# Order of the block loads in the feed-forward units, and two operand differences on VectorE

## The chip, the cores and the metric

The kernel runs on one core of a Trainium2 chip. The core has TensorE (matrix products), VectorE, ScalarE and GpSimd (elementwise work), SyncE (here only the queue that issues DMA transfers) and 16 DMA engines between HBM and the on-chip memory. The metric is the device time of one execution in microseconds.

## The reference, cut to what matters

The kernel computes one trunk layer of a decoder. 520 token columns (512 of a prompt, 8 of single-token sequences) go through norms, projections, two kinds of attention, and a feed-forward part. Only the last is touched by the change:

```python
D_MODEL = 2048
D_FF = 4 * D_MODEL
h = rmsnorm(x) * (1 + scale2) + shift2
x = x + gate2 * rmsnorm(relu(h @ w_ff1) ** 2 @ w_ff2)
```

All inputs are float32, and both matrix products are computed to nearly full float32 accuracy.

## The kernel before, in words

**Three matmuls for one product.** TensorE multiplies a shortened type. Each operand is therefore cut into a high part (ScalarE's cast) and a low part (the operand less its high part), and a block product is high·high + high·low + low·high: `mm3`, lines 445 to 447, matmuls of 128x128 by 260 columns. For weights the cut is `split_staged`: ScalarE casts (line 430, tile `wh`), ScalarE copies the block into PSUM (line 435, tile `stg`), VectorE subtracts (line 436, tile `wl`). For activations it is `split1` (lines 326 and 327, tiles `xf`).

**Units.** Most of both feed-forward products runs as units. A unit is a 2x2 block product done in seven block products rather than eight, by Strassen's scheme in Winograd's form. `PRODS` gives their order: P1 (weight A11), P5 (S1), P6 (S2), P3 (S4), P7 (S3), P2 (A12), P4 (A22). The A are 128x1024 blocks of weights (512 KB each); the S are sums of them, made by GpSimd in `wsum` (line 373):

S1 = A21 + A22, S2 = S1 − A11, S4 = A12 − S2, S3 = A11 − A21.

The other operand of each product is made of activations: B11, B22, B21 and T1 to T4, where T1 = B12 − B11, T2 = B22 − T1, T3 = B22 − B12, T4 = B21 − T2. Each product is 24 matmuls, a unit 168.

**Stages.** The first matrix has 28 units, two tiles of 128 output rows each; its result goes through relu and square (`ff1_unit`, tiles `fr`) to DRAM. The second matrix has 28 units, seven chunks of the hidden dimension with four units each (`ff2_unit`); an eighth chunk follows in a plain form. For a chunk, `form` loads four activation blocks from DRAM (line 2055, tiles `st`) and makes B and T (lines 2049 and 327). `form(0)` runs during the last unit of the first matrix; `form(c + 1)` runs step by step during chunk c.

**What sets the order.** Every engine runs its instructions in the order in which they were written. `drive` lists, for each unit, its four blocks (`items`), its sums (`sumq`) and its products (`subs`). `sub` is called once per product: it issues loads up to seven items ahead, then the sums that are due, then the cuts of the next products. Blocks of kind "unit" go into a pool of four buffers (`wr`), those of kind "more" into other slots (`wr2`; three in the second matrix). Both matrices list A11, A12 as "unit" and A21, A22 as "more". A load waits in SP's queue until its buffer has been read for the last time. In the second matrix A21's buffer is the one that the previous unit's S3 reads last; the buffers of the others are freed by ScalarE's cuts. `load_to(k + 3)` in `wsum` sees to it that all four blocks are issued before any sum is. `form` for c > 0 pins its instructions to their written place among the others (`keep_in_program_order`); `form(0)` doesn't.

Of the kernel before, what the change touches and what calls it, by code (L numbers as in the profile page):

```python
# [13 lines left out]
OP = mybir.AluOpType  # L14
# [53 lines left out]
RING = 6  # L68


PRODS = (("P1", "A11", "B11", 0, True), ("P5", "S1", "T1", 1, True), ("P6", "S2", "T2", 0, False),
         ("P3", "S4", "B22", 1, False), ("P7", "S3", "T3", 0, False), ("P2", "A12", "B21", 2, True),
         ("P4", "A22", "T4", 0, False))
# [163 lines left out]
class Kern:  # L237
# [92 lines left out]
    def drive(self, ops):  # L330

        self.items, self.subs, self.sumq = [], [], []
        for items, _ in ops:
            k = len(self.items)
            self.items += items
            if items and items[0][1] == "unit":
                for _, src, *_ in PRODS:
                    if src[0] == "S":
# [26 lines left out]

    def wsum(self, k, name):

        a, b, op = {"S1": (2, 3, OP.add), "S2": ("S1", 0, OP.subtract), "S3": (0, 2, OP.subtract),
                    "S4": (1, "S2", OP.subtract)}[name]
        self.load_to(k + 3)  # L370
        a, b = (self.sums[k, n] if isinstance(n, str) else self.raw[k + n] for n in (a, b))
        t = self.sums[k, name] = self.V1.tile([128, 1024], F32, name=name, tag="s")
        self.nc.gpsimd.tensor_tensor(t, a, b, op=op)  # L373

    def sub(self):

        i = self.isub
        k, _, _, now = self.subs[i]
        for d in (self.raw, self.sums):
            for key in [key for key in d if (key[0] if d is self.sums else key) < k]:  # L380
                del d[key]
        look = 7 if isinstance(now, str) else 4 if self.items[min(k + 4, len(self.items) - 1)][1] == "more" else 2
        self.load_to(k + (LOOK if self.items[min(k + LOOK, len(self.items) - 1)][1] == "ada" else look))
        while self.sumq and self.sumq[0][0] <= i + 2 + SL:
            _, ku, name = self.sumq.pop(0)
            self.wsum(ku, name)
        while self.icut < len(self.subs) and (self.icut <= i + 2 or self.ahead < 3):
            k, o, n, src = self.subs[self.icut]
            if src and self.icut > i and sum(self.held.values()) + self.need(n) > RING:
                break  # L390
            if self.icut > i and self.items[k][1] == "more" and not self.more:
                break
            if self.icut > i + 2 and self.items[k][1] == "ada":
                break
            if not src:
                self.load_to(k)
                self.cut[self.icut] = self.raw[k]
            else:
                if src is True or src[0] == "A":
                    k += 0 if src is True else ("A11", "A12", "A21", "A22").index(src)  # L400
                    self.load_to(k)
                    wr = self.raw[k][:, o:o + n]
                else:
                    wr = self.sums[k, src][:, o:o + n]
                self.held[self.icut] = self.need(n)
                if n > 512 and self.slot % 2:
                    self.slot = (self.slot + 1) % RING
                a = 512 * self.slot
                self.slot = (self.slot + (n + 511) // 512) % RING
                wh, wl = self.wh[:, a:a + n], self.wl[:, a:a + n]  # L410
                if n > 512 and self.stage:
                    self.split_staged(wr, wh, wl)
                else:
                    self.split1(wr, wh, wl)
                self.cut[self.icut] = (wh, wl)
                self.ahead += 1
            self.icut += 1
        self.isub += 1
        self.ahead -= bool(now)
        self.held.pop(i, None)  # L420
        return self.cut.pop(i)
# [1551 lines left out]
    def products(self, deep, done):  # L1973


        accs = {}
        for name, _, x, c, opens in PRODS:
            if opens:
# [13 lines left out]
    def ff1_unit(self, t):  # L1992
        def run():
# [17 lines left out]
            def done(name, acc):  # L2011
# [13 lines left out]

            self.products(True, done)
        w = self.I["wff1"]
        return [(w[t][:, :1024], "unit"), (w[t][:, 1024:], "unit"), (w[t + 1][:, :1024], "more"),
                (w[t + 1][:, 1024:], "more")], run

    def step_form(self, last=True):

# [11 lines left out]
    def form(self, c):  # L2044

        pin = self.tc.keep_in_program_order if c else lambda ins: ins

        def tt(*a, **k):
            pin(self.nc.gpsimd.tensor_tensor(*a, **k))  # L2049

        order = ((0, 0), (0, 1), (1, 1), (1, 0))
        st = []
# [24 lines left out]
        if c:  # L2077
            yield 3
        tt(b11, b12, b11, op=OP.subtract)
        if c:  # L2080
            yield 2
        t2 = self.V1.tile([128, 4, HF], F32, name="t2", tag="a")
        tt(t2, b22, b11, op=OP.subtract)
        if c:
            yield 2
        put("T1", b11, pool)
        if c:
            yield 3
        tt(b12, b22, b12, op=OP.subtract)
        if c:  # L2090
            yield 2
# [51 lines left out]
    def ff2_unit(self, c, g):  # L2143
# [19 lines left out]

            self.products(False, done)
        w = self.I["wff2"][c, g]
        return [(w[b], "unit" if b < 2 else "more") for b in range(4)], run

    def open_last(self):
        self.close_fc()
# [108 lines left out]
```

## Time and profile before

| | us |
|---|---|
| three runs | 2857.93, 2870.22, 2874.36 |
| median | 2870.22 |
| the profiled execution | 2863.88 |
| its span | 2862.2 |
| TensorE busy (share of the span) | 2689.3 (94%) |
| VectorE busy | 1691.0 (59%) |
| ScalarE busy | 1571.3 (55%) |
| GpSimd busy | 1141.2 (40%) |

The span runs from the first to the last instruction; the execution's own time holds 1.7 us more around it. The units of the first matrix begin at about 1557 us and end at about 2126, those of the second run from 2135 to 2738, and the plain chunk and the last norm end at 2862. The mean granted clock of TensorE is 0.975 of its full level of 2.4 GHz; at the lower level, 1.2 GHz, a matmul takes twice as long. A row of a timeline reads: start, duration, engine, line, operation, output and inputs, and in brackets the idle time before it with what ended it. Matmuls are pipelined: the distance of their starts is what one costs, not the duration shown.

### The profile page before, as it was taken

To read this page: it belongs to the slowest core of one execution; us is meant where nothing else is said; L and a number is where in the kernel's file an instruction comes from. 1 tells how busy PE (TensorE), PEld (TensorE's weight loads), DVE (VectorE), ACT (ScalarE), POOL (GpSimd) and SP (SyncE) were. 2 spreads that over 40 slices of the span, in tenths; PEclk is the share of its full clock that TensorE was granted. 3 is DMA by queue.
4 is the path that set the end of the run, shared out by engine and by line. 5 is a ranking of instruction groups with operands and counts; after the bars stand their busy time and mean duration, and the time that the engine had idled before them with its cause. 6 is when DMAs were issued, how large, how long until landed. Compare 5 with 4: busy or idle time off the path is not lost.

```text
span 2862.2 us, 56309 instructions
## 1 busy us (share of the span) xinstructions
PE 2689.3 (94%) x21584; PEld 2490.1 (87%) x21584; DVE 1691.0 (59%) x3336; ACT 1571.3 (55%) x2780; POOL 1141.2 (40%) x909
## 2 busy tenths in 40 slices
PE   6999998999999989899988999999989999999996
PEld 3589967788888878788978999999989999999996
DVE  4465483357594555623886555555565666665667
ACT  3134322234544434323565777777778777777773
POOL 0000011113113351301554665655667676776613
PEclk9999999999999999899998999999999999999998
DMA  7753456754445546677655434334342333323354
GB/s 259 284 172 78 123 183 200 223 184 140 159 155 166 177 144 199 198 245 262 232 170 177 145 118 143 124 136 137 127 153 92 119 120 143 123 98 139 131 181 155
DMA packets 195126, 466.15 MB, mean 163 GB/s; under 512 B 25609, under 2 KB 76170, under 8 KB 194858
## 3 DMA queue, kind: packets, MB, share of 16 engines
q1 hardware_dynamic: 165616, 421.83, 43.5%
q10 hardware_dynamic: 27194, 36.53, 4.3%
q0 software_dynamic: 2048, 4.21, 0.5%
q8 instruction: 170, 2.79, 0.4%
q14 instruction: 98, 0.80, 0.1%
HBM read 413.57 MB, written 48.91 MB: 162 GB/s over the span
## 4 chain that ended last, share of the span: by engine, by line
PE 53%; DVE 8%; POOL 6%; issue 5%; ACT 4%; DMA 4%; SPq 0%; ACTq 0%; POOLq 0%; DVEq 0%
PE acc L445 16%; PE acc L447 15%; PE acc L446 15%; POOL S L373 3%; DMA wr<-in_wff 2%; PE m L480 2%; DMA wr<-in_win 2%; ACT wh L430 2%; DVE wl L327 1%; POOL xf L327 1%; DVE wl L436 1%; ACT stg L435 1%; PE m L274 1%; PE m L1139 1%; POOL st L2049 1%
## 5 line engine op out<-in xcount | busy, mean ns | idle before, releaser
L436 DVE TENSOR_TENSOR wl<-stg,wh 128x512 fp32r<-128x512 f32 (+1 forms) x584 | 490.0, 867 | 407.8 <-ACT wh L430 396.4
L445 PE MATMUL acc<-hh,wh 128*128 128x260 f32 (+1 forms) x1984 | 587.0, 297 | 10.9 <-ACT hh L621 4.9
L446 PE MATMUL acc<-hl,wh 128*128 128x260 f32 (+1 forms) x1984 | 567.7, 287 | 0.4 <-DVE hl L622 0.4
L447 PE MATMUL acc<-hh,wl 128*128 128x260 f32 (+1 forms) x1984 | 565.2, 286 | 1.3 <-DVE wl L327 1.3
L445 PE MATMUL acc<-xf,wh 128*128 128x260 f32 x1824 | 521.1, 286 | 24.7 <-ACT stg L435 20.4
L326 ACT CAST wh<-wr 128x512 fp32r<-128x512 f32 (+1 forms) x478 | 284.1, 612 | 467.4 <-DMA wr<-in_win 220.4
L327 DVE TENSOR_TENSOR wl<-wr,wh 128x512 fp32r<-128x512 f32 (+1 forms) x478 | 353.5, 754 | 312.9 <-ACT wh L326 304.4
L447 PE MATMUL acc<-xf,wl 128*128 128x260 f32 x1824 | 518.5, 284 | 4.6 <-DVE wl L327 4.6
L446 PE MATMUL acc<-xf,wh 128*128 128x260 f32 x1824 | 518.3, 284 | 0.0
L445 PEld LDWEIGHTS acc<-hh,wh 128*128 128x128 f32 (+1 forms) x1984 | 376.0, 190 | 85.5 <-issue 45.5
L446 PEld LDWEIGHTS acc<-hl,wh 128*128 128x128 f32 (+1 forms) x1984 | 376.6, 190 | 8.0 <-DVE hl L622 4.5
L447 PEld LDWEIGHTS acc<-hh,wl 128*128 128x128 f32 (+1 forms) x1984 | 375.8, 190 | 5.9 <-DVE wl L327 4.4
L373 POOL TENSOR_TENSOR S<-wr,wr 128x1024 f32<-128x1024 f32 x112 | 276.4, 2469 | 252.7 <-DMA wr<-in_wff 170.9
L445 PEld LDWEIGHTS acc<-xf,wh 128*128 128x128 f32 x1824 | 346.7, 190 | 28.2 <-ACT stg L435 25.9
L447 PEld LDWEIGHTS acc<-xf,wl 128*128 128x128 f32 x1824 | 346.7, 190 | 4.9 <-DVE wl L327 4.9
L446 PEld LDWEIGHTS acc<-xf,wh 128*128 128x128 f32 x1824 | 346.6, 190 | 0.0
L435 ACT COPY stg<-S 128x512 f32<-128x512 f32 (+1 forms) x334 | 240.7, 731 | 106.2 <-DVE wl L436 73.1
L447 PE MATMUL acc<-h2h,wl 128*128 128x260 f32 x928 | 266.3, 287 | 8.8 <-DVE wl L327 8.7
L445 PE MATMUL acc<-h2h,wh 128*128 128x260 f32 x928 | 266.1, 287 | 6.2 <-ACT h2h L326 3.7
L446 PE MATMUL acc<-h2l,wh 128*128 128x260 f32 x928 | 266.4, 287 | 4.5 <-DVE h2l L327 4.5
L445 PE MATMUL acc<-T,wh 128*128 128x260 f32 x896 | 255.9, 286 | 11.6 <-DVE fr L2007 8.9
L447 PE MATMUL acc<-T,wl 128*128 128x260 f32 x896 | 256.0, 286 | 2.0 <-DVE wl L327 2.0
(538 smaller groups left out, 5800.8 us busy)
## 6 DMA issues: line engine op xcount, KB each, us to landing
wr<-in_wff SPq DMA_DIRECT2D x256, 512.0 KB, 4.8
wd<-in_wada SPq DMA_DIRECT2D x106, 512.0 KB, 4.7
wr<-in_win SPq DMA_DIRECT2D x106, 512.0 KB, 4.5
wr<-in_wada SPq DMA_DIRECT2D x86, 512.0 KB, 3.9
wr<-in_wout SPq DMA_DIRECT2D x48, 512.0 KB, 4.6
st<-f SPq DMA_DIRECT2D x32, 520.0 KB, 5.3
pg<-in_ckt SPq DMA_DIRECT2D x256, 64.0 KB, 2.7
wr<-in_wff2l SPq DMA_DIRECT2D x32, 512.0 KB, 3.5
```

The costliest lines, as they stand in the source:

```text
L274: self.nc.tensor.transpose(out, in_, self.ident[:n, :n])
L326: pin(self.nc.scalar.copy(hh, x))
L327: pin((eng or self.nc.vector).tensor_tensor(hl, x, hh.bitcast(F32), op=OP.subtract))
L373: self.nc.gpsimd.tensor_tensor(t, a, b, op=op)
L430: nc.scalar.copy(hh, x)
L435: nc.scalar.copy(p, x[:, s])
L436: nc.vector.tensor_tensor(hl[:, s], p, hh[:, s].bitcast(F32), op=OP.subtract)
L445: T.matmul(acc, wh[:, cs], xh, start=first, stop=False, skip_group_check=goes_on)
L446: T.matmul(acc, wh[:, cs], xl, start=False, stop=False, skip_group_check=goes_on)
L447: T.matmul(acc, wl[:, cs], xh, start=False, stop=last, skip_group_check=goes_on)
L480: self.nc.tensor.matmul(self.aacc[v][32 * g:32 * g + 32, :], self.cs[:, kt, :], w[:, j * 512:(j + 1) * 512], start=(kt == 0), stop=(kt == ...
L1139: nc.tensor.matmul(po[:, 0:256], vt[:, kb_ + k], pts[:, 256 * k:256 * k + 256], start=(kb_ + k == 0), stop=(kb_ + k == i))
```

## The change

It has two parts.

The four blocks of a unit are listed as A21, A22, A11, A12 instead of A11, A12, A21, A22, so that A21 and A22 go into the pool `wr` and A11 and A12 into the slots `wr2`. `UNIT` holds this order. A sum asks only for the blocks that it reads itself: `wsum` calls `load_to` with the larger index of its own blocks, no longer with the fourth.

In `form(0)` the first two differences, T1 = B12 − B11 and T2 = B22 − T1, go to VectorE instead of GpSimd. The third and fourth, and all of the later chunks, stay on GpSimd.

```diff
--- before.py
+++ after.py
@@ -68,6 +68,7 @@
 RING = 6
 
 
+UNIT = ("A21", "A22", "A11", "A12")
 PRODS = (("P1", "A11", "B11", 0, True), ("P5", "S1", "T1", 1, True), ("P6", "S2", "T2", 0, False),
          ("P3", "S4", "B22", 1, False), ("P7", "S3", "T3", 0, False), ("P2", "A12", "B21", 2, True),
          ("P4", "A22", "T4", 0, False))
@@ -365,10 +366,10 @@
 
     def wsum(self, k, name):
 
-        a, b, op = {"S1": (2, 3, OP.add), "S2": ("S1", 0, OP.subtract), "S3": (0, 2, OP.subtract),
-                    "S4": (1, "S2", OP.subtract)}[name]
-        self.load_to(k + 3)
-        a, b = (self.sums[k, n] if isinstance(n, str) else self.raw[k + n] for n in (a, b))
+        a, b, op = {"S1": ("A21", "A22", OP.add), "S2": ("S1", "A11", OP.subtract),
+                    "S3": ("A11", "A21", OP.subtract), "S4": ("A12", "S2", OP.subtract)}[name]
+        self.load_to(k + max(UNIT.index(n) for n in (a, b) if n in UNIT))
+        a, b = (self.raw[k + UNIT.index(n)] if n in UNIT else self.sums[k, n] for n in (a, b))
         t = self.sums[k, name] = self.V1.tile([128, 1024], F32, name=name, tag="s")
         self.nc.gpsimd.tensor_tensor(t, a, b, op=op)
 
@@ -397,7 +398,7 @@
                 self.cut[self.icut] = self.raw[k]
             else:
                 if src is True or src[0] == "A":
-                    k += 0 if src is True else ("A11", "A12", "A21", "A22").index(src)
+                    k += 0 if src is True else UNIT.index(src)
                     self.load_to(k)
                     wr = self.raw[k][:, o:o + n]
                 else:
@@ -2025,8 +2026,8 @@
 
             self.products(True, done)
         w = self.I["wff1"]
-        return [(w[t][:, :1024], "unit"), (w[t][:, 1024:], "unit"), (w[t + 1][:, :1024], "more"),
-                (w[t + 1][:, 1024:], "more")], run
+        return [(w[t + 1][:, :1024], "unit"), (w[t + 1][:, 1024:], "unit"), (w[t][:, :1024], "more"),
+                (w[t][:, 1024:], "more")], run
 
     def step_form(self, last=True):
 
@@ -2046,7 +2047,7 @@
         pin = self.tc.keep_in_program_order if c else lambda ins: ins
 
         def tt(*a, **k):
-            pin(self.nc.gpsimd.tensor_tensor(*a, **k))
+            pin((self.nc.gpsimd if c else self.nc.vector).tensor_tensor(*a, **k))
 
         order = ((0, 0), (0, 1), (1, 1), (1, 0))
         st = []
@@ -2086,6 +2087,8 @@
         put("T1", b11, pool)
         if c:
             yield 3
+        else:
+            tt = self.nc.gpsimd.tensor_tensor
         tt(b12, b22, b12, op=OP.subtract)
         if c:
             yield 2
@@ -2163,7 +2166,7 @@
 
             self.products(False, done)
         w = self.I["wff2"][c, g]
-        return [(w[b], "unit" if b < 2 else "more") for b in range(4)], run
+        return [(w[b], kind) for b, kind in ((2, "unit"), (3, "unit"), (0, "more"), (1, "more"))], run
 
     def open_last(self):
         self.close_fc()
```

Lines from 71 on have one number more after the change, those from line 2092 on three more.

**SP's queue in the second matrix, before.** The loads of two units, the second being the first of a chunk. The pairs `wr_27721`, `wr_27723` and `wr_27988`, `wr_27990` are A11 and A12; the pairs `wr2_27725`, `wr2_27727` and `wr2_27992`, `wr2_27994` are A21 and A22. The `st` are the activation blocks of the next chunk.

```order
L362 DMA wr_27721<-in_wff2 128x1024
L362 DMA wr2_27725<-in_wff2 128x1024
L362 DMA wr_27723<-in_wff2 128x1024
L362 DMA wr2_27727<-in_wff2 128x1024
L362 DMA wr_27988<-in_wff2 128x1024
L362 DMA wr2_27992<-in_wff2 128x1024
L2055 DMA st_27979<-f400_14719 128x1040
L2055 DMA st_27981<-f401_14720 128x1040
L362 DMA wr_27990<-in_wff2 128x1024
L2055 DMA st_27983<-f411_14722 128x1040
L2055 DMA st_27985<-f410_14721 128x1040
L362 DMA wr2_27994<-in_wff2 128x1024
```

The same stretch after the change, where `wr_27721`, `wr_27723` and `wr_27988`, `wr_27990` are A21 and A22, and the `wr2` are A11 and A12:

```order
L363 DMA wr_27723<-in_wff2 128x1024
L363 DMA wr2_27725<-in_wff2 128x1024
L363 DMA wr_27988<-in_wff2 128x1024
L363 DMA wr2_27727<-in_wff2 128x1024
L363 DMA wr_27990<-in_wff2 128x1024
L2056 DMA st_27979<-f400_14719 128x1040
L2056 DMA st_27981<-f401_14720 128x1040
L363 DMA wr2_27992<-in_wff2 128x1024
L2056 DMA st_27983<-f411_14722 128x1040
L2056 DMA st_27985<-f410_14721 128x1040
L363 DMA wr2_27994<-in_wff2 128x1024
```

Before, A21 of a unit (`wr2_27992`, which waits for the S3 of the unit ahead) stands in front of A12 and A22, and A11 in front of it. After, A22 (`wr_27990`) is the load that waits for that S3; A21 (`wr_27988`) stands ahead of it, and A11 and A12 behind it, A11 behind two operand loads and A12 behind four.

**VectorE at the hand-over from the first to the second matrix, before.** From the low part of one product to the addition that empties P7's accumulator (`acc0_24651`). `ft` and `fr` are the results of the first matrix, `xf` low parts of operands, `st` and `t2` operand blocks.

```order
L436 TENSOR_TENSOR wl_71<-stg_24741,wh_70 128x1024
L2000 COPY ft_24768<-acc0_24651 128x260
L436 TENSOR_TENSOR wl_71<-stg_24775,wh_70 128x1024
L327 TENSOR_TENSOR xf_24700<-st_24643,xf_24699 128x1040
L2007 TENSOR_TENSOR fr_24802<-acc1_24709,ft_24768 128x260
L327 TENSOR_TENSOR xf_24705<-t2_24697,xf_24704 128x1040
L327 TENSOR_TENSOR xf_24771<-st_24647,xf_24770 128x1040
L327 TENSOR_TENSOR xf_24807<-st_24645,xf_24806 128x1040
L436 TENSOR_TENSOR wl_71<-stg_24813,wh_70 128x1024
L2007 TENSOR_TENSOR fr_24802<-acc0_24651,ft_24738 128x260
```

After:

```order
L437 TENSOR_TENSOR wl_71<-stg_24741,wh_70 128x1024
L2050 TENSOR_TENSOR st_24643<-st_24645,st_24643 128x1040
L2001 COPY ft_24768<-acc0_24651 128x260
L2050 TENSOR_TENSOR t2_24697<-st_24647,st_24643 128x1040
L437 TENSOR_TENSOR wl_71<-stg_24775,wh_70 128x1024
L328 TENSOR_TENSOR xf_24700<-st_24643,xf_24699 128x1040
L2008 TENSOR_TENSOR fr_24802<-acc1_24709,ft_24768 128x260
L437 TENSOR_TENSOR wl_71<-stg_24813,wh_70 128x1024
L328 TENSOR_TENSOR xf_24705<-t2_24697,xf_24704 128x1040
L328 TENSOR_TENSOR xf_24771<-st_24647,xf_24770 128x1040
L2008 TENSOR_TENSOR fr_24802<-acc0_24651,ft_24738 128x260
```

The two differences of line 2050 stand among the copies and low parts, the second low part `wl` (`stg_24813`) has moved ahead of the split of T2, and the split of `st_24645` (the third difference) has moved behind P7's addition.

**GpSimd's sums of the first two units, before.**

```order
L373 TENSOR_TENSOR S1_18207<-wr2_18188,wr2_18205 128x1024
L373 TENSOR_TENSOR S2_18223<-S1_18207,wr_18184 128x1024
L373 TENSOR_TENSOR S4_18239<-wr_18186,S2_18223 128x1024
L373 TENSOR_TENSOR S3_18280<-wr_18184,wr2_18188 128x1024
L373 TENSOR_TENSOR S1_18405<-wr2_18276,wr2_18278 128x1024
L373 TENSOR_TENSOR S2_18440<-S1_18405,wr_18272 128x1024
```

After:

```order
L374 TENSOR_TENSOR S1_18205<-wr_18184,wr_18186 128x1024
L374 TENSOR_TENSOR S2_18223<-S1_18205,wr2_18188 128x1024
L374 TENSOR_TENSOR S4_18239<-wr2_18221,S2_18223 128x1024
L374 TENSOR_TENSOR S3_18280<-wr2_18188,wr_18184 128x1024
L374 TENSOR_TENSOR S1_18405<-wr_18272,wr_18274 128x1024
L374 TENSOR_TENSOR S2_18440<-S1_18405,wr2_18276 128x1024
```

The order of the sums is the same, S1, S2, S4, S3; what changes is the pools in which their blocks lie: S1 reads two tiles `wr`, S2 and S4 read a `wr2` each.

## Rows read from the trace of the kernel before

**Rows 1.** Busy time by stretch, us and (x instructions); PEclk is the granted clock.

```profile
1558.00:1571.00 13.00, 8.32 (x48) 7.90 (x48) 5.46 (x5) 6.22 (x8) 11.48 (x5) 0.74 0.30 107
1571.00:2130.00 559.00, 555.14 (x4628) 554.92 (x4626) 307.89 (x360) 419.58 (x498) 345.99 (x224) 1.00 0.40 135
2130.00:2141.00 11.00, 5.52 (x24) 5.27 (x24) 9.87 (x9) 6.31 (x10) 4.51 (x4) 0.53 0.47 169
2141.00:2740.00 599.00, 574.71 (x4713) 571.61 (x4714) 390.24 (x590) 462.14 (x650) 403.72 (x164) 0.99 0.33 124
```

**Rows 2.** Waits of TensorE from 2141 to 2740: us, times, longest.

```profile
PE acc L445 <- ACT stg L435: 20.4, 12, 4.3
PE acc L445 <- DVE f L2161: 3.8, 3, 1.9
```

**Rows 3.** Timeline of TensorE in a full stretch.

```profile
2143.30 0.28 PE L445 MATMUL acc<-xf,wh 128*128 128x260 f32 x1
2143.42 0.28 PE L446 MATMUL acc<-xf,wh 128*128 128x260 f32 x1
```

**Rows 4.** Timeline of GpSimd over one chunk of the second matrix.

```profile
2345.38 2.41 POOL L373 TENSOR_TENSOR S<-wr,wr 128x1024 f32<-128x1024 f32 x1 [6.36 <-DMA wr<-in_wff]
...
2393.13 3.42 POOL L373 TENSOR_TENSOR S<-wr,wr 128x1024 f32<-128x1024 f32 x1
2396.52 4.83 POOL L327 TENSOR_TENSOR xf<-st,xf 128x1040 fp32r<-128x1040 f32 x2
2409.50 2.40 POOL L373 TENSOR_TENSOR S<-wr,wr 128x1024 f32<-128x1024 f32 x1 [8.14 <-DMA wr<-in_wff]
...
2414.49 2.45 POOL L373 TENSOR_TENSOR S<-wr,S 128x1024 f32<-128x1024 f32 x1
...
2424.35 2.39 POOL L373 TENSOR_TENSOR S<-wr,wr 128x1024 f32<-128x1024 f32 x1
2433.14 2.40 POOL L373 TENSOR_TENSOR S<-wr,wr 128x1024 f32<-128x1024 f32 x1 [6.40 <-ACT stg L435]
```

**Rows 5.** Waits of GpSimd from 2141 to 2740: us, times, longest.

```profile
POOL S L373 <- DMA wr<-in_wff: 126.4, 21, 8.1
```

**Rows 6.** Timeline of the SP queue, second matrix: issue of block loads.

```profile
2426.77 1.75 SPq L362 DMA_DIRECT2D wr<-in_wff  x4
```

**Rows 7.** Timeline of GpSimd between two units of the first matrix.

```profile
1577.20 2.39 POOL L373 TENSOR_TENSOR S<-wr,wr 128x1024 f32<-128x1024 f32 x1
...
1583.73 2.40 POOL L373 TENSOR_TENSOR S<-wr,wr 128x1024 f32<-128x1024 f32 x1 [2.64 <-DMA wr<-in_wff]
```

**Rows 8.** Timeline of TensorE at the first unit.

```profile
1562.85 0.39 PE L445 MATMUL acc<-T,wh 128*128 128x260 f32 x1 [2.71 <-ACT wh L326]
...
1565.32 0.58 PE L447 MATMUL acc<-T,wl 128*128 128x260 f32 x1 [1.97 <-DVE wl L327]
```

**Rows 9.** Timeline of GpSimd at the first unit.

```profile
1559.37 2.35 POOL L373 TENSOR_TENSOR S<-wr,wr 128x1024 f32<-128x1024 f32 x1 [41.95 <-DMA wr<-in_wff]
```

**Rows 10.** Timeline of the SP queue ahead of the first unit.

```profile
1552.87 2.79 SPq L362 DMA_DIRECT2D wr<-in_wff  x4
```

**Rows 11.** Timeline of TensorE at the hand-over.

```profile
2135.03 0.56 PE L445 MATMUL acc<-T,wh 128*128 128x260 f32 x1 [8.89 <-DVE fr L2007]
```

**Rows 12.** Timeline of VectorE at the hand-over.

```profile
2118.57 1.23 DVE L436 TENSOR_TENSOR wl<-stg,wh 128x1024 fp32r<-128x1024 f32 x1 [0.29 <-ACT wh L430]
2122.59 2.52 DVE L327 TENSOR_TENSOR xf<-st,xf 128x1040 fp32r<-128x1040 f32 x1 [2.79 <-ACT xf L326]
...
2125.36 3.13 DVE L327 TENSOR_TENSOR xf<-t,xf 128x1040 fp32r<-128x1040 f32 x1
...
2134.47 0.41 DVE L2007 TENSOR_TENSOR fr<-acc,ft 128x260 f32<-128x260 f32 x1
```

**Rows 13.** Timeline of VectorE before the units: an operand split.

```profile
1530.24 1.24 DVE L327 TENSOR_TENSOR T<-y,T 128x1040 fp32r<-128x1040 f32 x1
```

## Prediction

> **What bounds the kernel now.** I read the table by stretch first [rows 1]. The 559 us between 1571 and 2130, where the units of the first feed-forward matrix run, are full: TensorE has no wait of over 0.1 us in them and the granted clock is 1.00 (the 4 us by which its busy time falls short hold missing matmul records). The loss lies beside them: 13 us at the first unit (clock 0.74), 11 us where the first matrix hands over to the second (0.53), and 599 us of the second matrix's units, busy for 574.7. The waits of TensorE in that last stretch are 20.4 + 3.8 us, most of them for ScalarE's staging copies [rows 2]. A unit is 168 matmuls that start 0.12 us apart in a full stretch [rows 3], so 20.2 us; 28 units want 564 us, and 599 were taken. From there I went to what feeds the copies. The timeline of GpSimd [rows 4] shows the loop: in each unit the sums S1, S2, S4, S3 run in this order at 2.4 to 3.4 us each, and after S3 GpSimd stands idle for about 6.4 us until the blocks for the next S1 have landed. Between the S1 at 2345.38 and the one at 2433.14 lie four units, one chunk: 87.8 us, against 80.6 us of matmuls. In the stretch 126.4 us of GpSimd's idle time are put down to block loads, 21 waits in 28 units [rows 5]. The SP queue says why: its four loads start at 2426.77, 0.03 us after the end of S3 (2424.35 + 2.39) [rows 4, 6]. The head of that group is A21 of the next unit, which takes the slot that S3 frees; A12 and A22 stand behind it, and S1 needs A22, the third. So loads and sums form a closed loop that is slower than TensorE.
>
> **Second matrix: the order of loads.** After the change A21 of a unit goes into the four-buffer pool and stands a unit earlier in the queue. A22 now waits for the previous S3 and heads the group; A11, A12 and the next A21 follow. S1 therefore waits for the first of a group instead of the third. What that wait then lasts is seen in the first matrix, where the last block for S1 already leaves alone at the head: S3 ends at 1577.20 + 2.39 = 1579.59, and S1 starts at 1583.73, 4.14 us later [rows 7], against 6.40 here [rows 4]. That is 2.3 us less for three units of a chunk.
> In the fourth, four loads of the next chunk's operands are in the same group, and S1 comes 13.0 us after S3 (2396.55 to 2409.50) with two splits of 4.83 us between. Now A22 is ahead of them and the splits cover it: S1 at about S3 + 4.9. S4 needs A12, still the last of the group, which I put where the last block lands now (about S3 + 13), so S4 starts at about 2409.9 instead of 2414.49: 4.6 us gained there. Sum per chunk: 3 x 2.3 + 4.6 = 11.5; the loop goes from 87.8 to about 76, under the 80.6 of TensorE. TensorE's waits should mostly go: 24.2 us [rows 2], and the clock lost behind them, 0.99 of 599, some 6 us (3 to 9 by rounding) [rows 1], together 30. The other account, 599 - 564, gives 35. I keep some 5 us of waits, since the operand splits still fall on VectorE and ScalarE in bunches, and take 25. Below, if A22 lands no sooner than now, the term is 0; above, 35. No sum, split or copy is added or removed: the same 2.4 us sums and the same loads. Every wait queued behind the new head was behind the old one too. The first matrix gains nothing: it has no wait to lose, and its S1 has the same gate before and after.
>
> **First unit.** P5 waits 2.71 and 1.97 us for the copy and the low part of S1 [rows 8]; S1 started at 1559.37 [rows 9], when A22 had landed, the second of the four loads issued from 1552.87 on [rows 10]. The half clock adds 13 x 0.26 = 3.4 us [rows 1]: 8.1 in all. After the change A21 and A22 have the places in the queue two groups earlier, so S1 is done before P5 asks. But A11, which P1 needs first, takes the first of the loads of 1552.87. The four are issued 0.7 us apart (2.79 / 4) [rows 10], so it lands 0.7 to 1.4 before 1559.37, say 1558.0; with a cast as long as VectorE's split of as many columns, 1.23 [rows 12], P1 starts at 1559.2. P1 ended at 1560.14 (1562.85 - 2.71), so with 24 x 0.12 it began at 1557.2: 2.0 us late, and its low part another 1 to 2 us later. New waits 3 to 4, half clock 2 to 3: a gain of 2, bounded by -1 (A11 lands no sooner than A22 did) and 5 (only the first wait is left).
>
> **Hand-over.** TensorE waits 8.89 us until 2135.03 for VectorE's addition that empties P7's accumulator [rows 11, 12]. That addition ran at 2134.47, in order behind VectorE's operand splits: 2.79 us of standing until ScalarE had cast T1, which waits for GpSimd's difference, then splits of 2.52 and 3.13 us and two more [rows 12]. With the two differences on VectorE the standing goes: the first stands ahead of the low part of 2118.57 [rows 12] and can run at about 2118. From there, in the new order: difference, copy 0.41, difference, low part 1.2, T1 split, addition 0.42, low part 1.2, T2 split, B22 split, then P7's addition. The five wide ones cost 1.24 alone [rows 13] and 2.52 to 3.13 beside a working GpSimd [rows 12]. GpSimd has two fewer to do there, so I take 1.9, in the middle: 2118 + 5 x 1.9 + 3.3 = 2130.8, 3.7 us earlier; 7.0 at 1.24, 0.7 at 2.5, and 2.5 us later at 3.13. Nothing hides this term: the wait is TensorE's own. The clock behind it (0.53 in 11 us) stays, as a wait of some 5 us remains. I take a gain of 4.
> The Trainium skill, "SBUF — State Buffer", section "Who interferes with whom", says that a VectorE instruction with two SBUF inputs and a GpSimd instruction that reads SBUF exclude each other and that the later one stands for the whole of the earlier. By it each of the five wide ones that meets a GpSimd instruction from its start would take 1.24 + 2.4 us (an estimate from the durations above), and the hand-over would lose 5 us rather than gain 4. The 2.52 and 3.13 of the row lie between no contention and that, so the trace agrees in direction and not in size.
>
> **The sum.** 25 + 2 + 4 = 31 us. The profiled execution took 2863.88 us (2862.2 span and 1.7 around it): 2833. It lies 6 us under the median of the three runs (2870.22, 2857.93 to 2874.36), so I say 2834 and let the range carry that spread.
>
> **Rivals.**
> *The loop keeps its length.* All loads go through the same 16 engines, and if four issued within 1.8 us [rows 6] land together, A22 at the head lands no sooner than as third. For it: the last loads beside the operands' are slow (13 us). Against it: 4.14 us in the first matrix, with two more loads right behind the one waited for [rows 7]. Only 6 us of the other terms are left: 2858.
> *A11 late (slower).* A11 used to be loaded a unit ahead; now it leaves after the previous S3. P1's copy stands three products (3 x 24 x 0.12 = 8.6 us) after P7's on ScalarE, which works in order. If A11 lands later than that, every later product of the unit is late. It decides from 8.6 us after S3 on, when S3 is only just in time. At each chunk's start, behind operand loads, it could land like the last load does, at 13: 4.4 us, with a quarter more for the clock (6 on 24, as above), in each of 7 chunks: 38 us, with the waits of today kept, so 2864 + 38 - 6 = 2896. Against it: A11 is third in that group, ahead of two of the four operand loads, and GpSimd gains a lead.
> *The hand-over turns worse.* The differences wait on VectorE for operand loads, and additions stand behind them. At 3.13 each and two more us for a late load: 4.5 lost instead of 4 gained: 2842.
> *All of it goes*, 35 + 8 + 9 us, if the lead covers every bunch: 2812.
> That the change does not do what it says is out for the order of loads, which the built order shows.
>
> **How the numbers follow.** A difference of 0.5% (14 us) is about what a measurement of this kernel can tell. Forecast 0.58 (2822 to 2846), all of it 0.10, hand-over worse 0.08: faster, 0.76. Loop keeps its length 0.16: within 0.5%. A11 late 0.08: slower. The range leaves out the slower case and the outer part of the best one: 2814 to 2860.
>
> **What would show it.** Right: GpSimd's idle time between S3 and S1 near 4 us in the second matrix; one load of a group ahead of the others by a unit; TensorE's waits for staging copies in that stretch under 8 us, its 28 units in about 570 us; the wait at the hand-over at 5 us instead of 8.9; P1 of the first unit 2 us later and P5 without a wait for S1. Wrong: S1 starting 6 us after S3 as before; ScalarE standing for A11; VectorE's differences at 3 us or more; new waits in the first matrix.

## The result and the profile after

The changed kernel took 2832.1 us (median of four runs, 2828.82 to 2836.97) against 2870.3 (four runs, 2857.93 to 2874.36): a ratio of 0.9874, 95% interval 0.9849 to 0.9899. The profiled execution took 2828.82 us with a span of 2827.1, 35.1 us less than that of before. The forecast was 2834, from 31 us on the profiled execution. The medians lie 38.2 us apart; the accounts below are of the two profiled executions.

The same stretches as in [rows 1], the last one cut where the units now end (length; busy time and, in brackets, instructions of TensorE, its weight loads, VectorE, ScalarE and GpSimd; granted clock; DMA share; GB/s):

```profile
1558.00:1571.00 13.00, 9.98 (x59) 9.48 (x59) 6.51 (x5) 7.37 (x10) 11.07 (x5) 0.74 0.52 173
1571.00:2130.00 559.00, 555.64 (x4628) 555.05 (x4627) 311.51 (x363) 421.31 (x500) 339.40 (x222) 1.00 0.41 137
2130.00:2141.00 11.00, 8.19 (x53) 7.83 (x54) 10.53 (x9) 5.68 (x9) 7.59 (x5) 0.84 0.12 45
2141.00:2703.00 562.00, 560.88 (x4673) 560.67 (x4673) 391.11 (x588) 460.99 (x648) 390.82 (x162) 1.00 0.37 131
```

The waits of TensorE in the units of the second matrix (us in total, times, longest):

```profile
PE acc L446 <- ACT f L2162: 1.1, 1, 1.1
```

Before, these waits were 24.2 us [rows 2]. One is left, besides 0.88 us just behind this window, at the start of the plain chunk, which is among the 24.2 of before. TensorE is busy for 560.88 of 562 us at full clock. It is now the engine that bounds this stretch.

Other waits, from TensorE's timeline (start, duration, engine, line, operation, tiles; in brackets the idle time before and what ended it), at the first unit, at the hand-over and at the first product of the second matrix:

```profile
1560.77 0.39 PE L446 MATMUL acc<-h2h,wh 128*128 128x260 f32 x1 [2.19 <-ACT wh L327]
...
1563.30 0.58 PE L448 MATMUL acc<-h2h,wl 128*128 128x260 f32 x1 [0.82 <-DVE wl L328]
...
2132.34 0.56 PE L446 MATMUL acc<-T,wh 128*128 128x260 f32 x1 [3.84 <-DVE fr L2008]
...
2144.62 0.39 PE L446 MATMUL acc<-xf,wh 128*128 128x260 f32 x1 [1.12 <-ACT f L2162]
```

Where the time came from, by places that both traces have. The first product P5 of the second unit starts at 1587.60 before and at 1587.59 after. Up to there nothing is gained on balance, but two things cancel: the last plain matmul ended 1.3 us later in this execution (1560.77 - 2.19 = 1558.58 against 1557.26), and the first unit gave 1.3 back. The 1.3 were there before any load of a unit is issued (1.35 at ScalarE's instructions around 1250 us), so the change has no part in them. The first matmul of the second matrix starts at 2141.02 before and at 2137.22 after: 3.8 us. The last unit ends (the start of the plain chunk) at 2738.96 and 2704.62, so the second matrix's units went from 597.9 to 567.4: 30.5 us. The rest, 0.7, lies behind. -1.3 + 1.3 + 3.8 + 30.5 + 0.7 = 35.0.

Now the loop that was forecast to open. GpSimd's timeline between two units of the second matrix, and SP's queue at that time:

```profile
2316.89 2.41 POOL L374 TENSOR_TENSOR S<-wr,wr 128x1024 f32<-128x1024 f32 x1
2323.07 2.41 POOL L374 TENSOR_TENSOR S<-wr 128x1024 f32<-128x1024 f32 x1 [3.77 <-DMA wr<-in_wff]
```

```profile
2319.32 1.75 SPq L363 DMA_DIRECT2D wr<-in_wff  x4
```

S3 ends at 2316.89 + 2.41 = 2319.30, four loads are issued from 2319.32 on, and S1 starts at 2323.07: 3.77 us after S3, where it had been 6.40 [rows 4, 6]. The group is as large as before and is issued as fast; only the block that S1 needs now stands first in it. Two units further on in the same chunk, S1 doesn't wait for a block at all:

```profile
2350.93 2.41 POOL L374 TENSOR_TENSOR S<-wr,wr 128x1024 f32<-128x1024 f32 x1
2359.53 2.40 POOL L374 TENSOR_TENSOR S<-wr 128x1024 f32<-128x1024 f32 x1 [6.19 <-ACT wh L431]
```

S1 at 2359.53 waits 6.19 us for ScalarE: the sums have four tiles, and the next one is free only when the older sum in it has been cut. GpSimd has run ahead as far as its tiles let it. Over the whole stretch its waits (us, times, longest) have changed hands. They were 126.4 us in 21 waits for blocks [rows 5] and are now

```profile
POOL S L374 <- ACT wh L431: 49.8, 19, 6.4
POOL S L374 <- ACT stg L436: 32.7, 13, 9.2
...
POOL S L374 <- DMA wr<-in_wff: 20.2, 6, 4.1
```

A wait for ScalarE's cut is the wait of a producer that is ahead; the waits for blocks were the ones that cost, and they are down to 20.2 us as the profile puts them down. (Five more S1, put down to ScalarE or TensorE for 8.9 us in all, start 3.7 us after S3 like those that wait for a block, so some of that may belong to the blocks too.)

VectorE at the hand-over, and GpSimd beside it:

```profile
2117.27 1.21 DVE L437 TENSOR_TENSOR wl<-stg,wh 128x1024 fp32r<-128x1024 f32 x1
2118.40 2.30 DVE L2050 TENSOR_TENSOR st<-st 128x1040 f32<-128x1040 f32 x1
...
2120.97 3.42 DVE L2050 TENSOR_TENSOR t<-st 128x1040 f32<-128x1040 f32 x1
...
2125.45 1.23 DVE L328 TENSOR_TENSOR xf<-st,xf 128x1040 fp32r<-128x1040 f32 x1
...
2128.07 2.20 DVE L328 TENSOR_TENSOR xf<-t,xf 128x1040 fp32r<-128x1040 f32 x1
2130.20 1.65 DVE L328 TENSOR_TENSOR xf<-st,xf 128x1040 fp32r<-128x1040 f32 x1
2131.78 0.41 DVE L2008 TENSOR_TENSOR fr<-acc,ft 128x260 f32<-128x260 f32 x1
```

```profile
2116.15 3.46 POOL L374 TENSOR_TENSOR S<-wr,wr 128x1024 f32<-128x1024 f32 x1
2120.84 2.46 POOL L2092 TENSOR_TENSOR st<-st 128x1040 f32<-128x1040 f32 x1 [1.23 <-DVE st L2050]
2126.76 2.42 POOL L2098 TENSOR_TENSOR st<-st,t 128x1040 f32<-128x1040 f32 x1 [3.46 <-DVE xf L328]
2129.14 1.61 POOL L2010 TENSOR_TENSOR fr<-fr 128x260 f32<-128x260 f32 x1
```

Each wide subtraction of VectorE here that reads two tiles `st`, `t` or `xf` (both in SBUF, the on-chip memory that GpSimd reads too) stands until GpSimd's current instruction has ended and then takes 1.1 us. The second difference starts at 2120.97; GpSimd's third difference runs from 2120.84 to 2123.30; 2123.30 - 2120.97 + 1.09 = 3.42. The first one: GpSimd's S3 ends at 2119.61, 1.21 us after 2118.40, and 1.21 + 1.09 = 2.30. The split of T2 at 2128.07: 1.11 + 1.09 = 2.20. That of B22 at 2130.20: GpSimd's multiplication ends at 2130.75, and 0.55 + 1.10 = 1.65. That of T1 at 2125.45 meets nothing and takes 1.23. The low part `wl` at 2117.27, which reads `stg` from PSUM, runs beside S3 and takes 1.21 all the same. The same sum explains the 2.52 and 3.13 of before [rows 12], with GpSimd's second and third differences of that trace beside them:

```profile
2121.54 2.47 POOL L2049 TENSOR_TENSOR t<-st 128x1040 f32<-128x1040 f32 x1
2123.95 3.44 POOL L2049 TENSOR_TENSOR st<-st 128x1040 f32<-128x1040 f32 x1
```

2121.54 + 2.47 is 1.42 after 2122.59, and 1.42 + 1.10 = 2.52; 2123.95 + 3.44 is 2.03 after 2125.36, and 2.03 + 1.10 = 3.13.

### The profile page after: what moved, and what is told of

It reads as the page before. It is cut to its first block, busy times and chain, and to the rows that moved or that the text cites. A ratio compares the mean times of both kernels' runs of the same rounds, so it can differ in the third digit from the quotient of the medians.

```text
span 2827.1 us, 56292 instructions
## 1 busy us (share of the span) xinstructions
PE 2681.5 (95%) x21584; PEld 2484.1 (88%) x21584; DVE 1693.7 (60%) x3338; ACT 1573.3 (56%) x2780; POOL 1127.3 (40%) x907
## 4 chain that ended last, share of the span: by engine, by line
PE 64%; DVE 6%; DMA 3%; issue 2%; ACT 2%; POOL 1%; SPq 0%; another core or an unknown queue 0%; ACTq 0%; DVEq 0%; POOLq 0%
PE acc L446 19%; PE acc L448 19%; PE acc L447 19%; DMA wr<-in_win 2%; PE m L481 2%; DVE wl L328 1%; PE m L275 1%; PE m L1140 1%; ACT wh L327 1%; PE m L1117 1%; ACT y L1901 0%; DVE cu L1301 0%; DMA rx<-mixd 0%; PE m L1482 0%; PE m L1639 0%
## 5 line engine op out<-in xcount | busy, mean ns | idle before, releaser
L446 PE MATMUL acc<-T,wh 128*128 128x260 f32 x896 | 254.5, 284 | 4.7 <-DVE fr L2008 3.8
L447 PE MATMUL acc<-T,wh 128*128 128x260 f32 x896 | 254.0, 283 | 0.0
```

Source lines behind the costliest of these rows:

```text
L446: T.matmul(acc, wh[:, cs], xh, start=first, stop=False, skip_group_check=goes_on)
L447: T.matmul(acc, wh[:, cs], xl, start=False, stop=False, skip_group_check=goes_on)
```

## The experiments

In all of them each item of a unit carries its block's name, so that sums and products find a block wherever it is listed. That alone leaves every engine's order as it is. The lists are `FF1` and `FF2` for the two matrices, `FIRST` and `SECOND` for the first two units; of each diff only the lines that matter are shown. Experiments 1, 3 and 4 are the kernel before but for the line shown, with each sum asking for its own blocks as in the changed kernel; these requests leave every engine's order as it is, too. 5 to 10 start from the changed kernel. Each ratio is against runs of the kernel before made beside it; the medians of those differ from group to group (2857 to 2870), so the ratios are what can be compared.

**1. The buffers alone, in the second matrix alone.**

```diff
-FF2 = (('A11', 'unit'), ('A12', 'unit'), ('A21', 'more'), ('A22', 'more'))
+FF2 = (('A11', 'more'), ('A12', 'more'), ('A21', 'unit'), ('A22', 'unit'))
```

> The second matrix alone, and of it the buffers alone: A11, A12, A21, A22 stay listed in this order, but A21 and A22 go into the four buffers and A11 and A12 into the three slots; the first matrix and the first chunk's differences as before. Theory (the gate: the last block that S1 needs must be the first load behind the wait for the previous S3; the buffers set the queue's order, not the list): TensorE has no wait of over 1.2 us in the units of the second matrix, a gain of about 32 us, 2863.88 - 32 = 2832 for a profile as early as that of before, ratio 0.988 to 0.991. First unit and hand-over as before (waits of 2.7 + 2.0 and 8.9 us). Rival 1 (the list's order or the sums' own requests bring the gain): ratio 0.997 to 1.003, waits of 20 us for staging copies as before. Rival 2 (the differences on VectorE give GpSimd the lead it needs): half of the waits stay, ratio 0.994.

2828.58 us against 2856.79; ratio 0.9893 (0.9861 to 0.9926). All of TensorE's waits from the first unit to the plain chunk:

```profile
PE acc L449 <- DVE fr L2011: 8.9, 1, 8.9
PE acc L449 <- ACT wh L329: 2.4, 1, 2.4
PE acc L451 <- DVE wl L330: 1.9, 1, 1.9
PE acc L449 <- DVE f L2167: 0.9, 1, 0.9
PE acc L449 <- ACT fr L2012: 0.5, 1, 0.5
```

First unit and hand-over are as before, and the second matrix has no wait left but the 0.9 at its end: 565.5 us from its first matmul to the plain chunk, against 597.9. The blocks are still listed A11, A12, A21, A22, and yet SP's queue in the built program has them in the order of the changed kernel (A21, the previous A12, A22, A11): a load goes into the queue when its buffer comes free, so the buffers make the order and the list doesn't. The sums' own requests don't either: the program with the requests of before has the same order on every engine. "Load the second row first" is done by the words "unit" and "more".

**2. The two differences alone.** Lists, buffers and requests of before (the expectation speaks of the changed requests, which make no difference to the order); `form` as changed, the third and fourth difference on GpSimd.

```diff
-            pin(self.nc.gpsimd.tensor_tensor(*a, **k))
+            pin((self.nc.gpsimd if c else self.nc.vector).tensor_tensor(*a, **k))
```

> Only the first chunk's two differences on VectorE (and each sum asking for its own blocks, which leaves the order of every engine as it was); lists and buffers as before. Theory: the hand-over alone changes. P7's addition ends its stand 2 to 3 us earlier (wait of 8.9 down to about 4, with new waits of about 1 each at the copy and the low part), the first matmul of the second matrix 3 to 4 us earlier, and the loop of the second matrix keeps its length (87 to 88 us for a chunk that had it), so at most 4 us of 2864 stay: ratio 0.997 to 1.001. Rival (the lead from the hand-over is what empties the waits of the second matrix): ratio below 0.995.

2856.26 against 2856.79; ratio 0.9985 (0.9969 to 1.0001). The waits of TensorE from the first unit to the plain chunk that show it:

```profile
PE acc L449 <- ACT stg L439: 17.7, 11, 3.5
PE acc L449 <- DVE fr L2011: 3.9, 1, 3.9
...
PE acc L451 <- DVE wl L440: 1.1, 1, 1.1
```

The hand-over moves as in the changed kernel (8.9 down to 3.9, with 1.1 new at a low part), and from the second unit's P5 to the first matmul of the second matrix it takes 549.3 us against 553.4. The second matrix keeps nearly all of its waits: its units take 595.5 us against 597.9. So the lead from the hand-over does not open the loop, and the two parts of the change add.

**3. A21 in the large pool, but A22 third behind the gate.** In the second matrix A12 and A21 are "unit", A22 and A11 "more".

```diff
-FF2 = (('A11', 'unit'), ('A12', 'unit'), ('A21', 'more'), ('A22', 'more'))
+FF2 = (('A12', 'unit'), ('A21', 'unit'), ('A22', 'more'), ('A11', 'more'))
```

> Second matrix alone: A21 and A12 in the four buffers, A22 and A11 in the slots. A21 is still in the large pool, but now it is the load that waits for the previous S3; A12 of the next unit, A22 and A11 stand behind it in the queue. Theory (the gate): S1 waits for the third load of its group again, GpSimd stands about 6 us between S3 and S1, and A11 comes fourth, so P1 may wait too: ratio 0.998 to 1.010. Rival (it is enough that A21 is in the large pool, or that A11 leaves it): ratio 0.988 to 0.992.

2842.59 against 2856.79; ratio 0.9952 (0.9934 to 0.997). Neither expectation was met: the loop came back, at a little over half of its old cost (583.3 us for the units, between 565.5 and 597.9). TensorE waits, and GpSimd stands before S1 as it did before the change:

```profile
PE acc L449 <- ACT stg L439: 11.0, 10, 2.7
```

```profile
2373.53 3.44 POOL L377 TENSOR_TENSOR S<-wr,wr 128x1024 f32<-128x1024 f32 x1
...
2385.88 2.40 POOL L377 TENSOR_TENSOR S<-wr,wr 128x1024 f32<-128x1024 f32 x1 [6.49 <-ACT stg L439]
...
2403.04 2.40 POOL L377 TENSOR_TENSOR S<-wr,wr 128x1024 f32<-128x1024 f32 x1
2411.88 2.40 POOL L377 TENSOR_TENSOR S<-wr,wr 128x1024 f32<-128x1024 f32 x1 [6.44 <-ACT stg L439]
```

From 2403.04 + 2.40 to 2411.88 are 6.44 us, as in [rows 4]. (The profile names a copy of ScalarE that ended last, there and here; most of the waits of this length it puts down to the loads.) What is better is the start of a chunk. S3 ends at 2376.97 and S1 starts at 2385.88, 8.9 us later, where it had been 13.0. SP's queue shows why: at that place A22 is the fourth load behind the gate (A21, two operand loads, A22), not the seventh.

```profile
2377.00 0.33 SPq L365 DMA_DIRECT2D wr<-in_wff  x1
2377.42 0.86 SPq L2059 DMA_DIRECT2D st<-f  x2
2378.33 0.42 SPq L365 DMA_DIRECT2D wr<-in_wff  x1
```

I had missed that when I wrote the expectation. So the distance from S3 to S1 goes with the place of the last block that S1 needs: 3.6 to 3.8 us as the first load, mostly 6.2 to 6.6 as the third, 11.5 to 13.0 as the seventh (the kernel before). As the fourth with two operand loads ahead it is less regular: 8.9 at three starts of a chunk, 7.5, 7.7 and 13.1 at the others. Place and bytes grow together here; no run separates them.

**4. An older gate.** In the second matrix A11 and A21 are "unit", A22 and A12 "more".

```diff
-FF2 = (('A11', 'unit'), ('A12', 'unit'), ('A21', 'more'), ('A22', 'more'))
+FF2 = (('A11', 'unit'), ('A21', 'unit'), ('A22', 'more'), ('A12', 'more'))
```

> Second matrix alone: A11 and A21 in the four buffers, A22 and A12 in the slots. The load that waits for an S3 is A11 of the unit after the next, and the S3 is one unit older; A22 of the next unit stands fourth behind it. Theory (the loop from S3 to the next S1 costs; a gate one unit older opens it as well, whatever stands where in the group): ratio 0.988 to 0.992, S1 not waiting for blocks. Rival (the position of A22 at the head of its group is what counts): ratio 0.997 to 1.005, GpSimd standing 6 us before S1.

2824.59 against 2856.79; ratio 0.9873 (0.9838 to 0.9908): as good as the changed kernel, though A22 stands fourth. No load that S1 needs waits for the S3 just ahead of it. GpSimd's timeline, an S3 and the S1 behind it:

```profile
2400.65 2.42 POOL L377 TENSOR_TENSOR S<-wr 128x1024 f32<-128x1024 f32 x1
2403.02 2.41 POOL L377 TENSOR_TENSOR S<-wr,wr 128x1024 f32<-128x1024 f32 x1
...
2415.61 2.41 POOL L377 TENSOR_TENSOR S<-wr,S 128x1024 f32<-128x1024 f32 x1 [2.94 <-DMA wr<-in_wff]
```

S1 (2403.02) starts when S3 (2400.65) ends; no block is waited for there. GpSimd now stands before S4 (2415.61), 2.94 us for A12, and TensorE doesn't feel it: of its waits in the units of the second matrix only the 0.9 at the end is left. So it is the loop that costs, S3 to load to the next S1; the head of the group is one way out of it and an older gate is another.

**5. The first unit: A11 in the large pool too.** The changed kernel with

```diff
-FIRST = (('A21', 'unit'), ('A22', 'unit'), ('A11', 'more'), ('A12', 'more'))
+FIRST = (('A21', 'unit'), ('A22', 'unit'), ('A11', 'unit'), ('A12', 'more'))
```

for the first unit alone.

> The changed kernel, with A11 of the very first unit in the four buffers too (A21, A22 and A11 there, only A12 in a slot). In the changed kernel A11 of that unit waits in its slot for the last plain tile's matmuls, and P1 waits 2.19 + 0.82 us, with 6.83 us of half clock behind. Theory (that wait is for the slot, not for the bytes): P1 of the first unit starts without a wait, 3.0 us and up to 3.4 us of clock less, against the changed kernel 3 to 6 us. Rival (the queue ahead of the first unit is full, and one load more in front makes another product of the unit late): the waits move to P2, whose block comes last, or to the second unit, gain under 1 us.

2834.47 against 2865.72; ratio 0.9887 (0.9864 to 0.9909), no better than the changed kernel. The wait for A11 went and a longer one came:

```profile
1565.08 0.39 PE L451 MATMUL acc<-h2h,wl 128*128 128x260 f32 x1 [0.22 <-DVE wl L330]
...
1575.81 0.56 PE L449 MATMUL acc<-T,wh 128*128 128x260 f32 x1 [4.94 <-DVE ft L2004]
```

P6 adds to the accumulator of P1, so it waits until VectorE has copied P1 out. The copy stands in VectorE's order behind the low parts of S2 and S4, ScalarE stood 3.74 us for S4 before it cast S2, and GpSimd had waited for S4's block A12:

```profile
1564.98 3.44 POOL L377 TENSOR_TENSOR S<-wr,S 128x1024 f32<-128x1024 f32 x1 [3.55 <-DMA wr<-in_wff]
```

A12 was now the block whose slot the last plain tile frees. From the last plain matmul to the second unit's P5 it took about 31 us instead of 29.0. It is the rival's case, a wait moved to another product, though the expectation had looked for it at P2 or in the second unit.

**6. Operands of the first chunk later.** The changed kernel with T2, B22 and the last two differences written after P7's addition:

```diff
+        if not c:
+            V, P = self.nc.vector.tensor_tensor, self.nc.gpsimd.tensor_tensor
+            V(b11, b12, b11, op=OP.subtract)
+            put("T1", b11)
+            yield 4
+            t2 = self.V1.tile([128, 4, HF], F32, name="t2", tag="a")
+            V(t2, b22, b11, op=OP.subtract)
+            put("T2", t2)
+            yield
+            put("B22", b22)
+            yield
+            P(b12, b22, b12, op=OP.subtract)
+            put("T3", b12)
+            yield
+            put("B21", b21)
+            P(b11, b21, t2, op=OP.subtract)
+            put("T4", b11)
+            return
```

> The changed kernel, with T2, B22 and the third and fourth differences of the first chunk written after P7's addition; only B11, T1 and the first two differences stay ahead of it on VectorE, and no difference of GpSimd lies beside the second one. Theory (P7's addition stands behind VectorE's wide instructions, and each of these stands until GpSimd's current instruction ends, then takes 1.1 us): the second difference takes 1.2 us instead of 3.42, the wait of 3.84 us goes, the waits of 0.82 and 1.04 shrink, the first matmul of the second matrix comes 4 to 7 us earlier than in the changed kernel. Rival (the operands moved back are then late for P5, P6 and P3 of the first unit of the second matrix): the wait reappears there, gain under 1.5 us.

2817.69 against 2865.72; ratio 0.9828 (0.9804 to 0.9852). P7's successor waits 0.30 us instead of 3.84, the clock stays full, and the way from the second unit's P5 to the first matmul of the second matrix is 545.8 us instead of 549.6. That is 3.9 us, just under the 4 to 7 expected, because 2.7 us are waited in front of that matmul where it had been 0.5. The second difference took 2.31 and not 1.2 us: GpSimd had begun its own difference first (a line each of VectorE and GpSimd).

```profile
2125.56 2.31 DVE L2089 TENSOR_TENSOR t<-st 128x1040 f32<-128x1040 f32 x1
```

```profile
2124.30 2.48 POOL L2094 TENSOR_TENSOR st<-st 128x1040 f32<-128x1040 f32 x1 [1.23 <-DVE st L2085]
```

2124.30 + 2.48 is 2126.78, that is 1.22 after 2125.56, and 1.22 + 1.09 = 2.31. The ratio lies some 13 us below that of the changed kernel, and the trace accounts for 3.9 of them; the intervals of the two ratios touch, so no more than the 3.9 is shown.

**7. 5 and 6 together.**

> Both edits on the changed kernel. Theory: the two stretches have nothing in common, so the gains add: 8 to 12 us less than the changed kernel, ratio to the kernel before 0.983 to 0.986. Rival (either edit brings nothing): 0.986 to 0.989.

2823.85 against 2865.72; ratio 0.986 (0.9841 to 0.988). The ratio lies on the border between the two forecasts; the trace decides for the rival: it has 5's new wait (4.93 us) and 6's gain (545.2 us on the same way).

**8. All four blocks of the first unit in the large pool**, on top of 6:

```diff
+FIRST = (('A21', 'unit'), ('A22', 'unit'), ('A11', 'unit'), ('A12', 'unit'))
+SECOND = (('A11', 'unit'), ('A12', 'unit'), ('A21', 'more'), ('A22', 'more'))
```

> The kernel with the late operands (T2, B22 and the last two differences after P7's addition), and in it the first unit's four blocks all in the four buffers; the second unit's A11 and A12 take the buffers as they come free and its A21 and A22 the slots; from the third unit on as in the changed kernel. Moving A11 alone had only moved the wait: A12, left in the slot, came late, and P6 waited 4.94 us for VectorE's copy. Theory (no block of the first unit may stand behind the slot that the last plain tile frees): no wait of over 0.5 us in the first unit, the stretch from the last plain matmul to the second unit's P5 about 26 us instead of 29 to 31, 3 us and up to 3 us of clock less than the kernel with late operands alone; ratio 0.980 to 0.983. Rival (the blocks of the second unit are then late, for their buffers are freed by the first): a new wait of 2 to 5 us in the second or third unit, ratio 0.983 to 0.986.

2814.44 against 2859.78; ratio 0.9845 (0.9821 to 0.9868). The first unit's waits are down to 1.14 and 0.20 us (0.5 at most was expected), with no half clock and no new wait behind; from the last plain matmul to the second unit's P5 it takes 24.9 us instead of 29.0. In the time of the whole kernel the gain does not stand out: the intervals of 6 and 8 overlap.

**9. 6 with the last two differences on VectorE as well** (`P(` becomes `V(` in its diff).

> The kernel with the late operands, with the third and fourth differences on VectorE as well, behind P7's addition. In the kernel with late operands the second difference still took 2.31 us: GpSimd had begun the third one 1.26 us earlier. Theory (a wide instruction of VectorE stands until GpSimd's current one ends and then takes 1.1): with no difference left on GpSimd the second one takes 1.1 to 1.25 us, P7's addition comes at least 1 us earlier and the first matmul of the second matrix 1 to 2 us earlier. Rival (it is slow because of what ScalarE, TensorE and the DMAs do at that time): it takes 2 us or more again.

2814.07 against 2859.78; ratio 0.984 (0.9819 to 0.9862). The second difference, with no difference of GpSimd beside it:

```profile
2115.96 1.23 DVE L2089 TENSOR_TENSOR t<-st 128x1040 f32<-128x1040 f32 x1
```

1.23 us, after 3.42 and 2.31. The wait behind P7's addition is gone, and the way to the second matrix is 543.9 us, 1.9 less than in 6.

**10. 8 and 9 together.**

> The last two together: all four blocks of the first unit in the four buffers, T2, B22 and the last two differences after P7's addition, all four differences on VectorE. Theory: nothing is shared, so what is left of TensorE's waits between 1550 and 2705 is 1.3 in the first unit, 0.8 and 1.4 at the hand-over, 0.9 at the end, together under 5 us, with no half clock in that stretch: ratio 0.980 to 0.984. Rival (the remaining differences between these kernels are smaller than what a measurement tells apart): 0.982 to 0.987 and no difference from either edit alone.

2809.43 (2805.9 to 2811.92) against 2858.17; ratio 0.9821 (0.9799 to 0.9842), where the changed kernel has 0.9849 to 0.9899. All that is left of TensorE's waits from the first unit to the plain chunk:

```profile
PE acc L452 <- DVE wl L331: 1.6, 2, 1.4
PE acc L450 <- ACT fr L2013: 1.4, 1, 1.4
PE acc L450 <- DVE f L2186: 0.9, 1, 0.9
PE acc L450 <- DVE ft L2005: 0.8, 1, 0.8
```

4.7 us, all at full clock, under the 5 expected. It beats both kernels; against 6, 8 and 9 alone the intervals overlap.

## Why the prediction was right

**Second matrix: 25 forecast, 30.5 measured.** The mechanism held: from the second chunk on, S1 came 3.6 to 3.8 us after S3 in two of a chunk's four units (4.1 forecast, from the first matrix), with four loads in the group as before, and the loop fell below TensorE's 80.6 us a chunk, so that TensorE sets the pace. In the other two units S1 came 5.2 to 6.4 and, at a chunk's start, 9.2 to 9.8 us after S3, where 4.1 and 4.9 had been reckoned. There GpSimd stood for ScalarE, which had yet to cut an older sum or to cast an operand, and not for a block. Experiment 1 gives 32.4 us with the buffers alone, experiments 3 and 4 put part of the loop back and open it in another way. The size was off in the sentence "I keep some 5 us of waits": one wait of 1.1 us remains. Once GpSimd gains on TensorE in every unit, its lead grows until the four tiles of the sums are full, and the bunches of operand work no longer reach TensorE. With the loop below the bound engine's pace nearly all of its waits went, and the clock lost behind them with them: the account 599 - 564 = 35 was the better one.

**Hand-over: 4 forecast, 3.8 measured, in part by luck.** P7's addition was to run at 2130.8 and ran at 2131.78. The matmul that waits for it started at 2132.34 instead of 2135.03, 2.7 us earlier where 3.7 were forecast, and from there to the second matrix it took 4.88 us instead of 5.99: 1.1 of clock, of which none was forecast. The five wide instructions were put at 1.9 each, 9.5 in all; they took 2.30 + 3.42 + 1.23 + 2.20 + 1.65 = 10.8. Not contention in general set these, but which of them met GpSimd. Three waits that I hadn't named came in: 0.82 and 1.04 us at the copy and the low part behind the differences, and 1.12 us at the second matrix's first copy, which counts against the 30.5 above. The clock was expected to stay at the 0.53 of before in these 11 us; 0.84 was granted. Two of the signs that the prediction names for being wrong did show: a difference of VectorE at 3 us or more (3.42), and new waits in the first matrix (0.82 and 1.04, in its last unit).

The Trainium skill, "SBUF — State Buffer", section "Who interferes with whom", names an exclusive lock, and the prediction said that the trace agreed in direction and not in size. That was wrong: it agrees in size as well. The one that comes later is blocked until the earlier one ends, so what is paid is the rest of GpSimd's instruction; I had priced each meeting as if it began with GpSimd's. Experiments 6 and 9 show it with the same instruction: 3.42, 2.31 and 1.23 us, as GpSimd's neighbour began just before it, 1.26 us before it, or not at all.

**First unit: 2 forecast, 1.3 measured.** P5 lost its wait for S1, P1 waits 2.19 us for A11 and 0.82 for its low part; 3 to 4 were forecast. The half clock stayed as long as before (0.74 granted in the same 13 us), where 2 to 3 us of loss had been reckoned instead of 3.4. At the lower clock matmuls start 0.22 us apart against 0.12 at the full one, so it costs somewhat less than the double that was reckoned with.

**The rivals.** The loop did not keep its length. A11 was never late: in the units of the second matrix ScalarE has no wait for a block. The hand-over did not turn worse. The sum, 31 of 35.1 us, was short mainly by the waits that were kept. That 2834 came within 2 us of the median is better than the terms deserve: the second matrix was 5.5 us short, and the median of the four runs after lies 3.3 above their profiled execution.

## What to carry to other kernels

Look for loops in which a buffer's last reader releases the load that the next of its kind waits for. As long as such a loop is longer than the bound engine's own work, its length and not any engine's busy share is the pace; count what stands between gate and need in the queue, and let the gated load be the last that the next reader still waits for, with nothing ahead of it in its group, or let the gate be one round older. Where such a loop falls under the bound engine's time, count nearly all of its waits as gained. And ask what GpSimd does beside work that is moved from it to VectorE: the same difference took 3.42 us beside it and 1.23 alone.

## What the runs showed of the chip that was not expected

The time of a wide VectorE subtraction with both operands in SBUF beside GpSimd is not a spread but a sum, rest of GpSimd's instruction plus 1.09 to 1.10 us, in the seven cases worked out above, of three kernels.

Stretches that the change can't reach move by several us: at the same ScalarE instruction the execution after the change was 8.6 us ahead of the one before at 734 us and 2.0 behind at 1450. One pair of spans would not have shown a term of 1 or 4 us; ways between marks within one trace did, and agreed over the kernels (553.4 and 553.5 us with the old hand-over, 549.3, 549.6 and 550.0 with the new one).
